# A two-layer decoder trunk on one core: half-height gate matmuls, weights loaded twice with a cast, and a spatial product of 256 columns

## The chip, the core and the metric

The kernel runs on one core of a Trainium2 chip. The metric is the device time of one execution, in microseconds (us). The kernel before was timed in three runs: 1560.33, 1560.44 and 1563.29 us, median 1560.44.

## What is computed

Two layers over x of 512 rows by 1024, in float32. Each layer adds half a SwiGLU feed-forward, a mixer, and half a second feed-forward, each behind an RMS norm. Layer 0 mixes with a recurrence, layer 1 with a spatial gate. Cut to the two mixers:

```python
def recurrent_mixer(x, w_in, conv_w, conv_b, ga_w, ga_b, gx_w, gx_b, lam, w_out):
    y, r = jnp.split(x @ w_in, 2, axis=-1)               # 1024 -> 2 x 1024
    y = jax.nn.gelu(y)
    r = causal_depthwise_conv(r, conv_w, conv_b)         # 4 taps
    gate_a = sigmoid(block_diag_linear(r, ga_w, ga_b))   # 16 heads of 64 x 64
    gate_x = sigmoid(block_diag_linear(r, gx_w, gx_b))
    log_a = -8 * gate_a * softplus(-lam)
    bx = r * gate_x * jnp.sqrt(-jnp.expm1(2 * log_a))
    h = scan(h[t] = exp(log_a[t]) * h[t-1] + bx[t])
    return (y * h) @ w_out

def spatial_gating_mixer(x, w_in, v_norm, w_s, b_s, w_out):
    u, v = jnp.split(jax.nn.gelu(x @ w_in), 2, axis=-1)
    v = rms_norm(v, v_norm)                              # 4 chunks of 128 rows, 8 heads of 128
    sg = jnp.einsum('hpq,bnqhc->bnphc', tril(w_s), vc) + b_s
    return (u * sg) @ w_out
```

## The kernel before, in words

`trunk` is written as one list of steps, the subs (`Sub`). A step takes one weight tile of 128x1024 from `rawp` (10 buffers, one load by SyncE, the SP queue), splits it into a high part `whi` (a copy by ScalarE, ACT, L117) and a low part `wlo` (a subtraction by VectorE, DVE, L108), and runs the tile's matmuls on TensorE, PE. Every product is three fp32r matmuls: high by high, high by low, low by high (`mm3`, L246 to L248, and `seven`, L481 to L483). `load_more` keeps the ten buffers filled, several steps ahead; a split runs three steps ahead of its matmuls (`SPLIT_AHEAD`). All other work is attached to a step by `hook(n, phase, fn)`, with the phases pre, mid, rest, end and late. Each engine executes its instructions in the order that results from this list. GpSimd (POOL) issues accumulating DMAs that add one weight block to another (L159).

**The recurrence** (`recurrent`). Steps r0 to r7 produce the channels of r, eight blocks of 128 rows by 512 columns; the first four are cut into halves of 256 columns. Steps y0 to y7 (`y0 = at0 + 12`) produce the channels of y. After each r step, `r_post` scales the product out of PSUM (`rc`, on ACT), adds three taps on DVE, and splits the result into `hi` (ACT) and `lo` (DVE). One or two steps later come the channel's gates: two blocks a and x, each a 128x128 weight tile with two 64x64 heads on its diagonal and zeros beside them, three matmuls of 512 columns each. Then two sigmoids of 128x512 and a tanh (ACT), and a product `pr` (DVE). `plan` places the rest: exponentials, `oma2`, square roots, scans, gelu, and `yh` = y * h, whose quarters form the left sides (A11, A12, S1 and so on) of the two groups of the output product `w_out`, which `seven` computes from seven block products P1 to Q4.

**The spatial mixer** (`spatial`). `prep_ws` loads the spatial weights 8 steps before the mixer and masks them (POOL); `tr_ws` turns them with eight PE transposes, and `take_ws` copies them out of PSUM (ACT). `v_norm` scales v with eight DVE operations of 128x512. `spat` multiplies: for each of 4 chunks and 2 halves of the heads four plain-float32 matmuls of 128 columns, 32 in all; the trace counts two passes for each. They stand in four groups of eight. `gated` adds the bias and multiplies by u.

Of the kernel before, what the change touches and what calls it, by code (L numbers as in the profile page):

```python
# [14 lines left out]
P = 128  # L15
# [21 lines left out]
SLOTS = 56  # L37

# [35 lines left out]
def trunk(ctx: ExitStack, tc: tile.TileContext, a: dict, out: bass.AP):  # L74
# [57 lines left out]
    class Raw:  # L132


        halves = False
# [36 lines left out]
    class Sub:  # L172
# [19 lines left out]
        def split(self, between=None):  # L192
# [4 lines left out]
            src = self.raw.v  # L197
            assert self.tile is None and self.raw.plus is None and self.raw.done == self.at[0]
# [1002 lines left out]
    def recurrent(w_in, w_out, norm):  # L1201
        gates = {}

        def load_gate(name, q):
            g = gates[name, q] = slot(name="gw")
            nc.gpsimd.memset(g, 0.0)
            gv = g.rearrange("p (c j) -> p c j", c=4)
            wv = a[f"rec_gate_{name}_w"][0, q * 8 : (q + 1) * 8].rearrange("(c two) i j -> two i c j", two=2)
            for two in range(2):
                nc.sync.dma_start(out=gv[two * 64 : (two + 1) * 64, :, two * 64 : (two + 1) * 64], in_=wv[two])  # L1210

        def split_gate(name, q):
            gates[name, q] = split(gates[name, q])
# [3 lines left out]
        for n, (name, q) in enumerate((name, q) for q in range(2) for name in ("a", "x")):  # L1217
            hook(at0 + (-9,-8,-2,-1)[n], "late", lambda name=name, q=q: load_gate(name, q))
            hook(at0 + (-3,-2,3,4)[n], "mid", lambda name=name, q=q: split_gate(name, q))
# [3 lines left out]
        def r_post(c, ps):  # L1223
            n = now[0]
            g = n + (2 if c < 4 or c == 6 else 1)
# [8 lines left out]
            def gate():  # L1234
                for name in "ax":
                    pg = bank("gate")
                    wh, wl = gates[name, c // 4]
                    cs = slice((c % 4) * P, (c % 4 + 1) * P)
                    mm3(pg, wh[:, cs], wl[:, cs], hl[0], hl[1], True, True)
                    pss.append(pg)  # L1240
                hl.clear()

            def sigmoids():
                for dst, brow in ((ga, V_GA), (gx, V_GX)):
                    dst[c] = slot(name="g")
                    act(dst[c], pss.pop(0), AF.Sigmoid, bias=vcol(brow + c))
# [8 lines left out]
            hook(n + 1, "mid", lambda: hl.extend(split(v)))  # L1255
# [53 lines left out]
        plan(-2, "rest", (exp_, 0, 1, 2, 3, 4), (oma2, 0, 1))  # L1309
# [31 lines left out]
        def mk(c0, post, halves):  # L1341

            raw = raw_of(w_in[:, c0 : c0 + P].rearrange("(k p) c -> p k c", p=P), [P, KD, P])
            st = {}
# [10 lines left out]
            last = lambda: post(st[0])  # L1355
# [22 lines left out]
    def spatial(w_in, w_out, norm):  # L1378
        wst, vg, v, sg = {}, {}, {}, {}
        ssv = cp.tile([P, 2 * TT], F32, tag="ssv", name="ssv")  # L1380

        def prep_ws():
            for q in range(2):
# [4 lines left out]
                                        fill=0.0, base=0, channel_multiplier=1)  # L1388
                vg[q] = slot(name="vg")
                nc.scalar.dma_start(out=vg[q], in_=a["sg_v_norm"][0, q * 512 : (q + 1) * 512].partition_broadcast(P))  # L1390
                wst[q] = w

        def tr_ws(q):
            ps = aux("wst")
            for i in range(4):
                nc.tensor.transpose(ps[:, i * P : (i + 1) * P], wst[q][:, i * P : (i + 1) * P], ident)
            wst[q] = ps

        def take_ws(q):
            wt = slot(name="wst")  # L1400
            act(wt, wst[q], AF.Copy)
            wst[q] = wt
# [58 lines left out]
        def v_norm(n):  # L1461
            for t in range(TT):
                stt(v[t, n], v[t, n], root["r"][:, t : t + 1], vg[n], ALU.mult, ALU.mult)

        def spat(t, n, where=None):

            ps = sg[t, n] = (where or aux)("sg")
            for i in range(4):
                c = slice(i * P, (i + 1) * P)
                nc.tensor.matmul(ps[:, c], wst[n][:, c], v[t, n][:, c], start=True, stop=True)  # L1470
# [8 lines left out]
        def gated(t, n):  # L1479
            ps, o = sg.pop((t, n)), hts[n][t]  # L1480
            for i in range(4):
                c = slice(i * P, (i + 1) * P)
                stt(o[:, c], ps[:, c], vcol(V_SB + n * 4 + i), o[:, c], ALU.add, ALU.mult)
            v.pop((t, n))
# [6 lines left out]
        hook(at0 - 8, "late", prep_ws)  # L1491
        for q in range(2):
            hook(at0 + 8 + q, "end", lambda q=q: tr_ws(q))
            hook(at0 + 9 + q, "mid", lambda q=q: take_ws(q))
# [5 lines left out]
        hook(u0 + 1, "mid", lambda: v_norm(0))  # L1500
        hook(u0 + 7, "mid", lambda: v_norm(1))
# [9 lines left out]
        for half, n, at, where in ((0, 0, 3, aux), (0, 1, 9, bank), (1, 1, 11, aux), (1, 0, 12, bank)):  # L1511
            for t in (2 * half, 2 * half + 1):
                hook(u0 + at, "end", lambda t=t, n=n, where=where: spat(t, n, where))
# [108 lines left out]
    def load_more(n=len(raws)):  # L1622
        nonlocal loaded
        while loaded < n and len(live) < RAW_BUFS:
# [181 lines left out]
```

## Time and profile before

| | |
|---|---|
| median of three runs | 1560.44 us |
| the profiled execution: its own time, and its span | 1560.53 us, 1558.5 us |
| PE busy | 1550.6 us, 99% of the span, 7277 matmuls |
| DVE busy | 1309.5 us, 84% |
| ACT busy | 1194.2 us, 77% |
| POOL busy | 244.5 us, 16% |
| granted TensorE clock | 1.0 |
| DMA | 311.58 MB, mean 200 GB/s |

A busy time counts the stretches in which at least one instruction of the engine is under way. Matmuls overlap, so a matmul's own duration (0.39 us for 512 columns) is longer than the step from one start to the next (0.23 us), and it is the step from start to start that one matmul adds to PE's time. The 40-slice picture of DMA use is lowest in three slices, 5, 3 and 3 tenths, at 142, 108 and 98 GB/s: these hold the recurrence.

### The profile page before, as it was taken

The numbers are of one execution on the slowest core, as the hardware profiler recorded it, in microseconds if no ns is written. First come the engines' busy times: TensorE is split into PE (matmuls) and PEld (weight loads), VectorE is DVE, ScalarE is ACT, GpSimd is POOL, SyncE is SP. The second block draws the span as 40 slices with busy tenths as digits, with TensorE's granted clock in tenths as the row PEclk, the third lists the DMA queues.
The fourth block names the chain that finished last, engine by engine and source line by source line (L and its number), as shares of the span: only waits on it lengthen the run. The fifth ranks groups of instructions, "written<-read, shape, count | busy, mean of one in ns | idle before, by whom it ended". The sixth has DMA issues, their size and how long they took to land.

```text
span 1558.5 us, 20998 instructions
## 1 busy us (share of the span) xinstructions
PE 1550.6 (99%) x7277; PEld 1317.1 (85%) x7277; DVE 1309.5 (84%) x1784; ACT 1194.2 (77%) x1785; POOL 244.5 (16%) x220
## 2 busy tenths in 40 slices
PE   9999999999999999999999999999999999999998
PEld 7888888898888998888889988888888889888886
DVE  6977789888999787789897877798979997777998
ACT  7877786668778868786787777867987877777856
POOL 2111112300021111112211111122211111111120
PEclk9999999999999999999999999999999999999999
DMA  9888898953395888899987887999978869898994
GB/s 316 187 189 192 188 219 223 232 142 108 98 236 136 191 198 198 187 235 223 232 209 180 191 203 185 230 218 235 252 191 216 203 140 218 197 206 184 241 232 137
DMA packets 272987, 311.58 MB, mean 200 GB/s; under 512 B 115456, under 2 KB 153456, under 8 KB 272880
## 3 DMA queue, kind: packets, MB, share of 16 engines
q1 hardware_dynamic: 218592, 211.06, 46.9%
q0 software_dynamic: 52496, 97.33, 37.1%
q10 hardware_dynamic: 1792, 1.84, 0.4%
q8 instruction: 57, 0.93, 0.2%
q14 instruction: 50, 0.41, 0.1%
HBM read 282.39 MB, written 2.10 MB: 183 GB/s over the span
## 4 chain that ended last, share of the span: by engine, by line
PE 98%; DVE 2%; DMA 0%; issue 0%; ACT 0%; DVEq 0%
PE A L483 15%; PE A L482 15%; PE A L481 15%; PE C L483 8%; PE C L481 8%; PE C L482 8%; PE B L482 4%; PE B L483 4%; PE B L481 4%; PE r L247 2%; PE r L248 2%; PE r L246 2%; PE Q L483 1%; PE Q L481 1%; PE Q L482 1%; PE p L961 1%
## 5 line engine op out<-in xcount | busy, mean ns | idle before, releaser
L108 DVE TENSOR_TENSOR wlo<-raw,whi 128x1024 fp32r<-128x1024 f32 (+2 forms) x567 | 651.1, 1152 | 210.6 <-ACT whi L117 207.0
L117 ACT ACTIVATE whi<-raw 128x1024 fp32r<-128x1024 f32 (+2 forms) x567 | 564.5, 1001 | 229.2 <-DVE raw L108 93.3
L481 PE MATMUL A<-whi,hi 128*128 128x512 f32 (+1 forms) x1104 | 420.8, 381 | 0.0
L482 PE MATMUL A<-whi,lo 128*128 128x512 f32 (+1 forms) x1104 | 419.3, 380 | 0.2 <-DVE lo L108 0.2
L483 PE MATMUL A<-wlo,hi 128*128 128x512 f32 (+1 forms) x1104 | 419.3, 380 | 0.0
L481 PEld LDWEIGHTS A<-whi,hi 128*128 128x128 f32 x1104 | 207.3, 188 | 35.9 <-ACT c L117 1.0
L482 PEld LDWEIGHTS A<-whi,lo 128*128 128x128 f32 x1104 | 207.3, 188 | 35.6 <-DVE lo L108 0.6
L483 PEld LDWEIGHTS A<-wlo,hi 128*128 128x128 f32 x1104 | 207.2, 188 | 35.7
L159 POOL DMA_DIRECT2D raw<-in_ffn_w_in_dram x100 | 120.7, 1207 | 708.8 <-DVE raw L108 322.8
L481 PE MATMUL C<-whi,hi 128*128 128x512 f32 (+1 forms) x608 | 231.5, 381 | 0.0
L483 PE MATMUL C<-wlo,hi 128*128 128x512 f32 (+1 forms) x608 | 231.3, 380 | 0.0
L482 PE MATMUL C<-whi,lo 128*128 128x512 f32 (+1 forms) x608 | 231.3, 380 | 0.0
L159 POOL DMA_DIRECT2D raw<-in_ffn_w_out_dram x73 | 83.8, 1189 | 319.0 <-DVE wlo L108 204.3
L108 DVE TENSOR_TENSOR raw<-raw,raw 128x1024 f32<-128x1024 f32 (+1 forms) x113 | 130.9, 1158 | 1.1
L482 PEld LDWEIGHTS C<-whi,lo 128*128 128x128 f32 x608 | 114.2, 188 | 20.2
L483 PEld LDWEIGHTS C<-wlo,hi 128*128 128x128 f32 x608 | 114.1, 188 | 19.9
L481 PEld LDWEIGHTS C<-whi,hi 128*128 128x128 f32 x608 | 114.1, 188 | 19.8
L117 ACT ACTIVATE c<-A 128x512 f32<-128x512 f32 (+1 forms) x150 | 81.8, 567 | 46.6 <-PE A L483 46.4
L108 DVE TENSOR_TENSOR lo<-a,hi 128x512 fp32r<-128x512 f32 (+1 forms) x180 | 116.3, 653 | 0.7 <-ACT hi L117 0.7
L117 ACT ACTIVATE hi<-a 128x512 fp32r<-128x512 f32 (+1 forms) x180 | 105.5, 596 | 14.4 <-DVE a L108 12.6
L482 PE MATMUL B<-whi,lo 128*128 128x512 f32 (+1 forms) x304 | 115.8, 381 | 0.0
L481 PE MATMUL B<-whi,hi 128*128 128x512 f32 (+1 forms) x304 | 115.7, 381 | 0.0
(190 smaller groups left out, 1973.5 us busy)
## 6 DMA issues: line engine op xcount, KB each, us to landing
raw<-in_ffn_w_in_dram SPq DMA_DIRECT2D x143, 512.0 KB, 5.5
raw<-in_ffn_w_out_dram SPq DMA_DIRECT2D x98, 512.0 KB, 5.7
raw<-in_ffn_w_in_dram POOLq DMA_DIRECT2D x76, 512.0 KB, 7.5
raw<-in_ffn_w_out_dram POOLq DMA_DIRECT2D x58, 512.0 KB, 8.4
raw<-in_ffn_w_in_dram SPq DMA_DIRECT2D x48, 384.0 KB, 4.0
raw<-in_sg_w_in_dram SPq DMA_DIRECT2D x20, 512.0 KB, 8.6
raw<-in_ffn_w_in_dram POOLq DMA_DIRECT2D x24, 384.0 KB, 6.4
raw<-in_rec_w_in_dram SPq DMA_DIRECT2D x16, 512.0 KB, 5.3
```

Of the source, the lines that this page charges most:

```text
L108: nc.vector.tensor_tensor(out=o, in0=x, in1=y, op=op)
L117: nc.scalar.activation(out=o, in_=x, func=f, **k)
L159: nc.gpsimd.dma_start(out=self.v, in_=src, accum_op=ALU.add)
L246: nc.tensor.matmul(ps, wh, xh, start=start, stop=False)
L247: nc.tensor.matmul(ps, wh, xl, start=False, stop=False)
L248: nc.tensor.matmul(ps, wl, xh, start=False, stop=stop)
L481: nc.tensor.matmul(ps, zh, wh, start=fresh and i == 0, stop=False, **k)
L482: nc.tensor.matmul(ps, zl, wh, start=False, stop=False, **k)
L483: nc.tensor.matmul(ps, zh, wl, start=False, stop=end, **k)
L961: nc.tensor.matmul(bank_of(half, s), z, (sub.lo if m == 2 else sub.hi)[:, q, :], start=left[2] == "2" and (h, q, m) == (0, 0, 0), stop=lef ...
```

## The change

Three edits, with two tables of places.

1. *Gates.* One tile holds, for four channels, gate a on the diagonal blocks and gate x on the off-diagonal blocks, so the POOL memsets go, and two tiles are split instead of four. The 64 rows of a head are now one matmul's whole contraction: per channel six matmuls of 64 rows by 128 columns of weights, 512 moving columns each, the two row halves alternating and each with a PSUM bank of its own. Four sigmoids of 64x512 replace two of 128x512. Gates run 3 steps after r0 to r3 and 2 steps after r4 to r7 (`GATE`). In `plan`, the first exponentials come one step later, the last three exponentials, square roots and scans later by a phase or two.
2. *Casting loads.* Each of the 12 unhalved weight tiles of the recurrence (r4 to r7, y0 to y7) is loaded a second time by a POOL DMA that casts it to fp32r. That is its high part; ACT makes no `whi`. Such a tile takes two of the ten buffers.
3. *Spatial.* The spatial weights are loaded and masked 90 steps before the mixer, and turned by `Group.send`: four ACT copies into planes, two transposing DMAs on SP, two ACT merges. `v_norm` writes tiles with two chunks side by side, in sixteen operations of 128x256, at `V_AT`; `spat` has 16 matmuls of 256 columns instead of 32 of 128.

```diff
+GATE = (3, 3, 3, 3, 2, 2, 2, 2)
+V_AT = 1, 7, 9, 10
+WS_AT, WS_MERGE = 90, 8
...
+            if self.cast:
+                self.h = rawp.tile([P, 1024], F32R, tag="raw", name=nm("rawhi")).rearrange("p (k c) -> p k c", k=k)
+                live.add((self, "hi"))
+                nc.gpsimd.dma_start(out=self.h, in_=self.src)
...
+            if self.raw.cast:
+                self.hi = self.raw.h
...
+                tt(self.lo, src, f32(self.hi), ALU.subtract)
...
-            g = n + (2 if c < 4 or c == 6 else 1)
+            g = n + GATE[c]
...
-                for name in "ax":
-                    pg = bank("gate")
-                    wh, wl = gates[name, c // 4]
-                    cs = slice((c % 4) * P, (c % 4 + 1) * P)
-                    mm3(pg, wh[:, cs], wl[:, cs], hl[0], hl[1], True, True)
-                    pss.append(pg)
+                pss.extend(bank("gate") for _ in range(2))
+                cs = slice((c % 4) * P, (c % 4 + 1) * P)
+                for m in range(3):
+                    for two in range(2):
+                        rows = slice(two * 64, (two + 1) * 64)
+                        nc.tensor.matmul(pss[two], gates[c // 4][m == 2][rows, cs], hl[0][m == 1][rows, :],
+                                         start=m == 0, stop=m == 2)
...
-                for dst, brow in ((ga, V_GA), (gx, V_GX)):
-                    dst[c] = slot(name="g")
-                    act(dst[c], pss.pop(0), AF.Sigmoid, bias=vcol(brow + c))
+                for dst, brow, n in ((ga, V_GA, 0), (gx, V_GX, 1)):
+                    g = dst[c] = slot(name="g")
+                    for two in range(2):
+                        o = (two ^ n) * 64
+                        act(g[two * 64 : (two + 1) * 64], pss[two][o : o + 64], AF.Sigmoid, bias=vcol(brow + c)[o : o + 64])
...
-        plan(-2, "rest", (exp_, 0, 1, 2, 3, 4), (oma2, 0, 1))
+        plan(-1, "rest", (exp_, 0, 1, 2, 3, 4), (oma2, 0, 1))
...
-        plan(1, "late", (exp_, 5, 6, 7), (oma2, 5, 6, 7))
-        plan(2, "rest", (sqrt, 5, 6, 7))
-        plan(2, "late", (gelu, 0, 1, 2), (scan, 5, 6, 7))
+        plan(2, "rest", (exp_, 5, 6, 7), (oma2, 5, 6, 7))
+        plan(2, "late", (sqrt, 5, 6, 7))
+        plan(2, "late", (gelu, 0, 1, 2))
+        plan(3, "rest", (scan, 5, 6, 7))
...
+            raw.cast = not halves
...
-                nc.tensor.transpose(ps[:, i * P : (i + 1) * P], wst[q][:, i * P : (i + 1) * P], ident)
...
+                g, cs = Group(2), slice(2 * k * P, 2 * (k + 1) * P)
+                pairs[k] = g
+                g.send("ws", lambda q, cs=cs: wst[q][:, cs], (now[0] + 1 + k, "mid"), (now[0] + WS_MERGE + k, "mid"))
...
-                nc.tensor.matmul(ps[:, c], wst[n][:, c], v[t, n][:, c], start=True, stop=True)
...
+                for i in range(2):
+                    nc.tensor.matmul(o[:, i], ws(n, 2 * j + i), x[:, i], start=True, stop=True)
...
-        while loaded < n and len(live) < RAW_BUFS:
+        while loaded < n and len(live) < RAW_BUFS - raws[loaded].cast:
```

PE, the gates of the first channel. Before, three matmuls into each of the two gate banks, one bank after the other:

```order
L246 MATMUL gate_3463<-hi_3394,hi_3112 128x512
L247 MATMUL gate_3463<-lo_3395,hi_3112 128x512
L248 MATMUL gate_3463<-hi_3394,lo_3113 128x512
L246 MATMUL gate_3467<-hi_3394,hi_3134 128x512
L247 MATMUL gate_3467<-lo_3395,hi_3134 128x512
L248 MATMUL gate_3467<-hi_3394,lo_3135 128x512
```

Now the two banks alternate, and one pair of weight tiles serves both:

```order
L1256 MATMUL gate_3481<-hi_3379,hi_3110 128x512
L1256 MATMUL gate_3482<-hi_3379,hi_3110 128x512
L1256 MATMUL gate_3481<-lo_3380,hi_3110 128x512
L1256 MATMUL gate_3482<-lo_3380,hi_3110 128x512
L1256 MATMUL gate_3481<-hi_3379,lo_3111 128x512
L1256 MATMUL gate_3482<-hi_3379,lo_3111 128x512
```

ACT, from the gates of channels 3 and 4 to the conv scaling (`rc`) of channel 7; `g` is a gate, `tl` the tanh. Before:

```order
L117 ACTIVATE g_3656<-gate_3628,vec 128x512
L117 ACTIVATE g_3658<-gate_3632,vec 128x512
L117 ACTIVATE tl_3660<-g_3656,lru_c 128x512
...
L117 ACTIVATE hi_3668<-rc_3644 128x512
L117 ACT_TABLE_LOAD
...
L117 ACTIVATE rc_3718<-r_3685,vec 128x512
L117 ACTIVATE whi_3723<-raw_3116 128x1024
```

In this excerpt from before, `rc_3718` is channel 6, and one more channel's sigmoids stand between it and channel 7. Now the scaling that follows the table load and the five exponentials is channel 7's, and no `whi` follows it:

```order
L120 ACTIVATE g_3678<-gate_3653,vec 64x512
L120 ACTIVATE g_3678<-gate_3654,vec 64x512
L120 ACTIVATE g_3681<-gate_3653,vec 64x512
L120 ACTIVATE g_3681<-gate_3654,vec 64x512
L120 ACTIVATE tl_3684<-g_3678,lru_c 128x512
...
L120 ACTIVATE hi_3694<-rc_3669 128x512
L120 ACT_TABLE_LOAD
...
L120 ACTIVATE rc_3746<-r_3713,vec 128x512
```

PE, the spatial product of one chunk before, with its four heads printed as one row:

```order
L1470 MATMUL sg_11026<-c_2298_10588,wst_10802 128x128 x4
```

and now the same four heads for two chunks, where `vp` is v with two chunks side by side:

```order
L1508 MATMUL sg_11031<-vp_10970,ws_8748 128x2x128 x2
L1508 MATMUL sg_11034<-vp_10973,ws_8768 128x2x128 x2
```

Twice as many columns stand in one matmul, and half as many matmuls in a group.

## Rows read from the trace of the kernel before

**Rows 1.** The page: busy time by engine, and the chain that ended last.

```profile
PE 1550.6 (99%) x7277; PEld 1317.1 (85%) x7277; DVE 1309.5 (84%) x1784; ACT 1194.2 (77%) x1785; POOL 244.5 (16%) x220
...
PE 98%; DVE 2%; DMA 0%; issue 0%; ACT 0%; DVEq 0%
```

**Rows 2.** Windows: us, busy us (x) of PE, PEld, DVE, ACT, POOL; clock, DMA share, GB/s.

```profile
340.00:380.50 40.50, 40.50 (x236) 35.82 (x236) 32.10 (x47) 31.79 (x50) 1.21 (x1) 1.00 0.34 94
380.50:441.00 60.50, 60.50 (x269) 50.09 (x268) 58.81 (x84) 43.84 (x59) 6.05 (x5) 1.00 0.47 115
441.00:457.00 16.00, 16.00 (x72) 13.26 (x71) 15.52 (x21) 9.56 (x14) 3.62 (x4) 1.00 0.94 213
```

**Rows 3.** Timeline of PE, first gate group: start us, us, engine, line, op, out<-in.

```profile
351.11 0.28 PE L247 MATMUL r<-zl,whi 128*128 128x256 f32 x1
...
351.35 0.40 PE L246 MATMUL gate<-hi,hi 128*128 128x512 f32 x1
352.50 0.39 PE L248 MATMUL gate<-hi,lo 128*128 128x512 f32 x1
352.73 0.28 PE L246 MATMUL r<-zh,whi 128*128 128x256 f32 x1
```

**Rows 4.** Timeline of PE, where r6 has ended.

```profile
377.46 0.39 PE L246 MATMUL gate<-hi,hi 128*128 128x512 f32 x1
```

**Rows 5.** Timeline of ACT, from the gates of channels 3 and 4 on.

```profile
371.13 1.25 ACT L117 ACTIVATE g<-gate,vec 128x512 f32<-128x512 f32 x2
372.27 0.73 ACT L117 ACTIVATE tl<-g,lru_c 128x512 f32<-128x512 f32 x1
372.88 1.27 ACT L117 ACTIVATE g<-gate,vec 128x512 f32<-128x512 f32 x2
...
374.64 0.64 ACT L117 ACTIVATE hi<-rc 128x512 fp32r<-128x512 f32 x1
375.30 1.28 ACT L117 ACT_TABLE_LOAD   x1
376.59 3.18 ACT L117 ACTIVATE g<-g,lru_nc 128x512 f32<-128x512 f32 x5
379.68 0.76 ACT L117 ACTIVATE rc<-r,vec 128x512 f32<-128x512 f32 x1
380.34 1.05 ACT L117 ACTIVATE whi<-raw 128x1024 fp32r<-128x1024 f32 x1
```

**Rows 6.** Timeline of DVE, where channel 7 begins.

```profile
383.83 1.29 DVE L108 TENSOR_TENSOR pr<-rc,g 128x512 f32<-128x512 f32 x2
...
385.80 2.32 DVE L114 SCALAR_TENSOR_TENSOR rc<-r,vec,rc 128x509 f32<-128x509 f32 x3
```

**Rows 7.** Timeline, left side S1 of the second output group.

```profile
440.15 0.68 DVE L108 TENSOR_TENSOR lo<-a,hi 128x512 fp32r<-128x512 f32 x1
...
441.61 0.39 PE L482 MATMUL C<-whi,lo 128*128 128x512 f32 x1
```

**Rows 8.** Timeline of PE, transposes of half the spatial weights.

```profile
1131.78 0.60 PE L1396 MATMUL wst<-ident,ws 128*128 128x128 f32 x4
...
1132.44 0.40 PE L482 MATMUL C<-whi,lo 128*128 128x512 f32 x1
```

**Rows 9.** Timeline of PE, one group of the spatial product.

```profile
1157.21 1.95 PE L1470 MATMUL sg<-c,wst 128*128 128x128 f32 x16
...
1159.22 0.40 PE L482 MATMUL C<-whi,lo 128*128 128x512 f32 x1
```

**Rows 10.** DMA issues: KB each, median us from issue to landing.

```profile
raw<-in_ffn_w_out_dram POOLq DMA_DIRECT2D x58, 512.0 KB, 8.4
...
raw<-in_rec_w_in_dram SPq DMA_DIRECT2D x16, 512.0 KB, 5.3
```

**Rows 11.** Lines by form, POOL: busy us, mean ns, idle before.

```profile
L159 POOL DMA_DIRECT2D raw<-in_ffn_w_in_dram x100 | 120.7, 1207 | 708.8 <-DVE raw L108 322.8
...
L1387 POOL TENSOR_SCALAR_AFFINE_SELECT ws<-ws 128x512 f32<-128x512 f32 x2 | 1.5, 760 | 13.1 <-DMA ws<-in_sg_w_s_dram 13.1
```

More of the change, by code (lines that the diff above doesn't have):

```diff
@@ L132, in trunk @@
     class Raw:
-        halves = False
+        halves = cast = False
         def __init__(self, src, shape, plus=None, wait=2):
@@ L1202, in recurrent, with load_gate, split_gate @@
         gates = {}
-        def load_gate(name, q):
-            g = gates[name, q] = slot(name="gw")
-            nc.gpsimd.memset(g, 0.0)
+        def load_gate(q):
+            g = gates[q] = slot(name="gw")
             gv = g.rearrange("p (c j) -> p c j", c=4)
[L1208 to L1213, printed above, removed]
+            for n, name in enumerate("ax"):
+                wv = a[f"rec_gate_{name}_w"][0, q * 8 : (q + 1) * 8].rearrange("(c two) i j -> two i c j", two=2)
+                for two in range(2):
+                    o = (two ^ n) * 64
+                    nc.sync.dma_start(out=gv[two * 64 : (two + 1) * 64, :, o : o + 64], in_=wv[two])
+        def split_gate(q):
+            gates[q] = split(gates[q])
         at0 = len(subs)
         y0 = at0 + 12
-        for n, (name, q) in enumerate((name, q) for q in range(2) for name in ("a", "x")):
-            hook(at0 + (-9,-8,-2,-1)[n], "late", lambda name=name, q=q: load_gate(name, q))
-            hook(at0 + (-3,-2,3,4)[n], "mid", lambda name=name, q=q: split_gate(name, q))
+        for q in range(2):
+            hook(at0 + (-9, -2)[q], "late", lambda q=q: load_gate(q))
+            hook(at0 + (-3, 3)[q], "mid", lambda q=q: split_gate(q))
         rc, ga, gx, tl, pr, ym = {}, {}, {}, {}, {}, {}
@@ L1254, in r_post @@
             hook(n, "late", taps)
[L1255 removed]
+            hook(n + 1, "mid", lambda: hl.append(split(v)))
             hook(g, "end", gate)
@@ L1353, in mm_of, with last @@
                 return mm
-            last = lambda: post(st[0])
+            def last():
+                live.discard((raw, "hi"))
+                post(st[0])
             if not halves:
@@ L1378, in spatial @@
     def spatial(w_in, w_out, norm):
-        wst, vg, v, sg = {}, {}, {}, {}
+        wst, vg, v, sg, pairs, vp = {}, {}, {}, {}, {}, {}
         ssv = cp.tile([P, 2 * TT], F32, tag="ssv", name="ssv")
@@ L1490, in spatial @@
         at0 = len(subs)
[L1491 to L1494, printed above, removed]
+        hook(at0 - WS_AT, "late", prep_ws)
+        hook(at0 - 8, "late", load_vg)
+        hook(at0 - WS_AT + 6, "late", planes_ws)
         seven_chunk(D, v_done, ((2, 3), (3, 4), (2, 3)))
@@ L1499, in spatial @@
         hook(u0 + 1, "pre", v_newton)
-        hook(u0 + 1, "mid", lambda: v_norm(0))
-        hook(u0 + 7, "mid", lambda: v_norm(1))
+        for (half, n), at in zip(((0, 0), (0, 1), (1, 1), (1, 0)), V_AT):
+            hook(u0 + at, "mid", lambda half=half, n=n: v_norm(half, n))
         def drop(name):
@@ L1511, in spatial @@
         for half, n, at, where in ((0, 0, 3, aux), (0, 1, 9, bank), (1, 1, 11, aux), (1, 0, 12, bank)):
+            hook(u0 + at, "end", lambda half=half, n=n, where=where: spat(half, n, where))
             for t in (2 * half, 2 * half + 1):
-                hook(u0 + at, "end", lambda t=t, n=n, where=where: spat(t, n, where))
                 hook(u0 + at + 2, "mid", lambda t=t, n=n: gated(t, n))
@@ L1655, in vec_rest @@
             flat = src.rearrange("h d -> (h d)") if len(src.shape) == 2 else src.rearrange("o h d -> (o h d)")
-            nc.gpsimd.dma_start(out=stage[r0 : r0 + n, :P], in_=flat.rearrange("(n p) -> n p", p=P))
+            v = flat.rearrange("(n p) -> n p", p=P)
+            if r0 == V_GX:
+                for o in (0, 64):
+                    nc.gpsimd.dma_start(out=stage[r0 : r0 + n, o : o + 64], in_=v[:, 64 - o : 128 - o])
+            else:
+                nc.gpsimd.dma_start(out=stage[r0 : r0 + n, :P], in_=v)
     def vec_rest_t():
```

56 lines of the change are left out of this document (36 added, 20 removed).

## Prediction

> **What bounds the kernel now.** I read the page first. PE is busy for 99% of the span, and the chain that ended last is 98% PE [rows 1]: the reader is to see that, over the whole, an instruction taken from PE's queue is time taken from the kernel. But that is an average over stages, and the largest edit lies in one of them. So I cut the recurrence into windows [rows 2]. From 340 to 380.5 us DVE is busy for 32.10 of 40.50 us; from 380.5 to 441 for 58.81 of 60.50, and then until 457 for 15.52 of 16.00. PE never stops there, but DVE is at 97%. So two engines set the pace side by side in the second half of the recurrence, and the margin between them decides what a faster PE is worth. I take the margin from the timeline at the end of that stretch [rows 7]: the `lo` of the block S1 of the second output group starts on DVE at 440.15 and lasts 0.68, so it is there at 440.83; PE reads it at 441.61. The margin is 0.78 us. This is the number on which the forecast turns.
>
> **Gates on PE.** Each channel's six matmuls run from 351.35 to 352.73 [rows 3]: 1.38 us, 0.23 each. Now they are three pairs, and the halves of a pair use different rows of the array and different PSUM banks. No row of this trace shows such a pair. The bounds: together, a pair takes one matmul's 0.23; one after the other, 0.46. I take 0.24, near the lower end, because the two halves share neither weights, nor moving rows, nor a bank. Then a channel takes 0.72 instead of 1.38, and eight channels give back 5.3 us of PE's queue. Against it stands the overhang of a matmul: the last of the group lasts 0.39 but is followed after 0.23 [rows 3]. If the array had to empty wherever 128-row and 64-row matmuls meet, each meeting would cost up to that 0.16; there are seven places with gates in the new order, so 14 meetings and 2.2 us.
>
> **What becomes of the 5.3 us.** They are saved before and inside the stretch that DVE paces, so I follow DVE's work. Its last long run starts with the taps of channel 7 at 385.80 [rows 6] and goes on without a gap of note to the end of that `lo` at 440.83: 55.0 us. The new order has the same operations in this run and two more products `pr`, since the products of channels 6 and 7 now come after the taps. Two of them were 383.83 to 385.13, by their 1.29 us less the overlap about 0.6 each [rows 6], so 1.2 us more. So the question is when the taps of channel 7 start. They need its scaling `rc` on ACT, which lasts 0.76 [rows 5], so it must start some 0.8 us before them. The new order puts that `rc` directly behind this run on ACT: four sigmoids and a tanh of channel 3, the same of channel 4, `hi`, a table load, five exponentials. The run starts with the gates of channel 3, which stand behind r6. r6 ended at 377.46 [rows 4], behind five channels' gates; now three stand before it, so it ends at 377.46 - 5 x 1.38 + 3 x 0.72 = 372.7, and the gates of channel 3 are out of PE at 372.7 + 0.72 + 0.16 = 373.6. The durations from ACT's starts [rows 5]: a sigmoid 0.57 (371.13 to 372.27 is two), the tanh 0.61, `hi` 0.66, the table load 1.29, five exponentials 3.09. A sigmoid over 64 partitions has the same 512 columns, and I give it the same 0.57. Sum: 2 x (4 x 0.57 + 0.61) + 0.66 + 1.29 + 3.09 = 10.8, so `rc` of channel 7 starts at 384.4 and the taps at 385.2, 0.6 earlier than before. Then 385.2 + 55.0 + 1.2 = 441.4 for the `lo` of S1, against the 441.61 at which PE read it before. PE arrives 5.3 us earlier, at about 436.3, and **waits some 5 us**. What the recurrence gains is about 0.2 us, and behind it DVE is still at 97% [rows 2], so PE cannot run ahead there either.
>
> The rest of this edit: ACT gets 16 sigmoids more (9.2 us) and loses 12 `whi` of some 0.95 to 1.05 us [rows 5], 12 us. Nothing beside the run above hangs on it. DVE loses two splits of gate tiles, before 380.5, where it had 8.4 us to spare [rows 2]: nothing. The POOL memsets wait for nobody. The exponentials and scans of channels 5 to 7 are among the operations counted.
>
> **Casting loads.** They take `whi` from ACT, and DVE keeps its `wlo`, so DVE's stretch is not shortened. Their cost is in queues. An SP load of a tile of this stage lands in 5.3 us, an accumulating load that POOL issues in 8.4 [rows 10], at an issue of 1.2 us [rows 11]. A casting load lies between these two or above. It is issued about six steps ahead and needed at the split, three steps ahead; a step has 24 matmuls of 0.23 [rows 3], 5.5 us, so there are 16 us. DMA has room there, a share of 0.34 and 0.47 [rows 2]. Cost nothing; the cover ends where a cast takes over 16 us.
>
> **Spatial weights.** Four transposes on PE lie between 1131.78 and the second matmul behind them, 1132.44 [rows 8]; take off that first matmul's 0.23, and they cost 0.43. Twice that goes: **-0.87 us**, on PE's own queue in a stage where PE sets the pace. The masked load moves 82 steps ahead; POOL waited 13.1 us for its two loads there already [rows 11], with no step of the chain on POOL [rows 1], so I price the same wait in the same kind of feed-forward at nothing. ACT has six operations for two, at 0.6 to 1.05 each by its rows [rows 5] some 2.4 to 4.2 us over a whole feed-forward layer in which it is idle for a quarter: nothing.
>
> **Spatial product.** A group of 16 passes runs from 1157.21 to 1159.22 less 0.23 [rows 9]: 1.78 us, 0.111 a pass; four groups, 7.1 us. Afterwards there are 32 passes of 256 columns. The lower bound is a 256-column pass of fp32r, 0.12 (351.11 to 351.35 is two) [rows 3]: 32 x 0.12 = 3.8, a gain of 3.3. The upper bound is twice today's pass: 32 x 0.222 = 7.1, no gain. A pass of 128 plain float32 columns lasts as long as nearly 256 of fp32r, so plain float32 goes at half the rate by columns, and I take **zero**. The scaling of v is split into 16 operations of half the width: on DVE's rows of 128x512, 0.68 [rows 7], at most 5.4 us more, over a stage of ten steps of the mixer; DVE is idle for 16% overall [rows 1]. Nothing.
>
> A rule speaks for more. The Trainium skill ("TensorE: Matmul & The Clock Gate", LDWEIGHTS) says that loading weights of P columns takes about P/1.2 ns; by an estimate from that page, 107 ns for 128 columns, and the trace's 0.111 a pass agrees with it. By that rule the load sets the pace of today's passes, and the sum would be 1556.2 rather than 1559.5; rival 2 works it out from rows.
>
> **Sum.** The profiled execution took 1560.53 us: 1560.53 - 0.87 (transposes) - 0.2 (recurrence) - 0 (casts) - 0 (product) = 1559.46. It stands 0.09 above the median of the three runs, so the forecast is **1559.5 us**.
>
> **Rivals.**
>
> 1. *DVE's margin is larger than I read it*, since DVE's order also changes, and the `wlo` of 12 tiles no longer wait for an ACT copy. For it: DVE has 1.7 us idle between 380.5 and 441 [rows 2]. Against it: its run from 385.80 has no room for 5 us. Then PE's whole saving counts: 1560.5 - 5.3 - 0.9 = 1554.3. Chance 0.13.
> 2. *The weights' load sets the pace of a spatial pass.* A pass then costs its weights' load, whatever its columns; the 256-column pass costs 0.12 [rows 3], and 3.3 us go: 1556.2. For it: the transposes, with one pass each, step at the same 0.11 [rows 8]. Against it: 512 columns of fp32r take 0.23 and 256 take 0.12 [rows 3], and the same loads at 0.12 give half the columns in plain float32. Chance 0.10.
> 3. *The 64-row matmuls cost more.* If the array empties at each meeting, r6 ends and the gates come out 7 x 0.16 = 1.1 later (the gates of channels 0 to 2 and the entry to channel 3), the taps and the `lo` of S1 too: 442.5, 0.9 behind 441.61, and 1560.53 + 0.9 - 0.9 = 1560.5. If the pairs run one after the other, r6 ends at 377.46 - 2 x 1.38 = 374.7, the first gates are out at 376.2, 2.6 later than forecast, the `lo` of S1 at 444.0, 2.4 behind: 1562.1. The Trainium skill ("TensorEngine Tiling (Array Packing)", Key Properties) says that a change of the tiling mode drains TensorE; no row of the trace shows a change of mode. Chance 0.13 for both.
> 4. *Slower: the casting loads are late.* Each takes a POOL issue and two of ten buffers, and the twelve come one after another on one queue. The point is 16 us from issue to landing, or 5.5 us of POOL per load. Beyond that each step waits: at 1 us in each of the eight y steps, where DVE has no room to make it up, 1559.5 + 8 = 1567.5. For it: POOL's own loads land later than SP's [rows 10]. Against: 8.4 us is half of 16, and DMA stands at less than half. Chance 0.06.
>
> **How the numbers follow.** The forecast has 0.58, with a range of its own from 1558.6 to 1560.5 (half of DVE's 1.7 us of idle time on one side, an ACT run that is a tenth longer than 10.8 us on the other). A measurement of this kernel can tell 0.2%, 3.1 us, from no change. Rivals 1 and 2 lie below 1557.3: faster 0.23. Rival 4 lies above 1563.6, and so does a small part of rival 3: slower 0.07. Within: 0.70. The range leaves out rivals 1 and 4, 0.19 in all, and takes in 2 and 3: 1556.0 to 1562.3.
>
> **What would show it.** Each step has its row in the changed kernel's trace: a gate group on PE that takes some 0.72 us for a channel; r6's end near 372.7; the taps of channel 7 near 385.2; waits of PE in the last y step and in the first products of the output, summing to 4 to 5 us, ended by DVE; the read of S1 near 441.4; no `wst` transposes; a spatial group of 1.78 us. The forecast is wrong if PE reads S1 of the second group before 440, if the waits of PE end on a DMA, or if a spatial group takes a microsecond.

## The result, and the profile after

The changed kernel takes 1563.75 us, median of 19 runs (1561.68 to 1572.66), against 1560.52 for the kernel before (19 runs, 1559.89 to 1563.29): a ratio of 1.0027, 95% interval 1.0018 to 1.0035. It is slower by 4.2 us by the ratio, 3.2 by the medians. The forecast was 1559.5, its range ended at 1562.3, and slower had a chance of 0.07. The profiled execution took 1565.62 us, its span is 1563.9.

First the page of the changed kernel: busy time, and the chain that ended last.

```profile
PE 1550.4 (99%) x7237; PEld 1310.4 (84%) x7237; DVE 1309.2 (84%) x1790; ACT 1197.0 (77%) x1791; POOL 253.5 (16%) x229
...
PE 89%; DVE 6%; ACT 2%; DMA 1%; issue 1%; POOL 0%; DVEq 0%; POOLq 0%; ACTq 0%
```

PE is busy for as long as before [rows 1], and the span is 5.4 us longer. The chain, 98% PE before, now has 6% DVE and 2% ACT in it. The waits of PE in the changed kernel say where (engine, tile, line, what it waited for: us in total, times, longest):

```profile
PE r L262 <- DVE wlo L111: 2.1, 1, 2.1
PE C L495 <- ACT hi L120: 1.7, 1, 1.7
...
PE Q L495 <- ACT whi L120: 0.9, 1, 0.9
PE C L496 <- DVE lo L111: 0.6, 1, 0.6
PE Q L497 <- DVE wlo L111: 0.5, 1, 0.5
```

`r L262` is step y7, `C` is the block with S1. Waits were forecast at both places, 4 to 5 us in all and ended by DVE, and they come to 4.3 us. The longer of the two at S1 ends on ACT, whose `hi` had itself waited for DVE, as the timeline below shows. Two things were not forecast. The windows, as [rows 2]:

```profile
340.00:380.50 40.50, 40.50 (x243) 34.04 (x242) 31.91 (x44) 27.63 (x44) 4.38 (x5) 1.00 0.58 121
380.50:441.00 60.50, 58.43 (x260) 46.28 (x259) 54.83 (x79) 46.51 (x65) 6.66 (x7) 1.00 0.71 176
441.00:457.00 16.00, 13.75 (x53) 10.65 (x52) 14.51 (x20) 8.04 (x11) 5.86 (x5) 0.89 1.08 246
```

DVE is *less* busy in the second half, 54.83 us against 58.81: it was waiting for ACT at the start of that stretch, and its work slid past 441. Its rows there show it (in brackets the idle time before an instruction, and what ended it); the last is the taps of channel 7:

```profile
382.38 0.69 DVE L111 TENSOR_TENSOR lo<-rc,hi 128x512 fp32r<-128x512 f32 x1 [3.58 <-ACT hi L120]
...
384.41 0.69 DVE L111 TENSOR_TENSOR a<-g 128x512 f32<-128x512 f32 x1 [1.34 <-ACT g L120]
...
387.53 2.32 DVE L117 SCALAR_TENSOR_TENSOR rc<-r,vec,rc 128x509 f32<-128x509 f32 x3 [0.37 <-ACT rc L120]
```

And the granted clock of the last window is 0.89. The timeline at S1:

```profile
442.46 0.63 ACT L120 ACTIVATE hi<-a 128x512 fp32r<-128x512 f32 x1 [1.17 <-DVE a L111]
...
443.14 0.50 PE L495 MATMUL C<-whi,hi 128*128 128x512 f32 x1 [1.67 <-ACT hi L120]
...
443.48 0.68 DVE L111 TENSOR_TENSOR lo<-a,hi 128x512 fp32r<-128x512 f32 x1
...
444.22 0.73 PE L496 MATMUL C<-whi,lo 128*128 128x512 f32 x1 [0.57 <-DVE lo L111]
...
444.75 0.63 PE L497 MATMUL C<-wlo,hi 128*128 128x512 f32 x1
...
445.18 0.63 PE L495 MATMUL C<-whi,hi 128*128 128x512 f32 x1
```

The `lo` of S1 is there at 444.16, not 441.4; PE reads it at 444.22, where before it read it at 441.61 [rows 7]. And after the two waits the matmuls step by 0.43 us instead of 0.23: the half clock, 1.2 GHz (the granted clock is 0.50 from 445 to 447 us).

Compared matmul by matmul with the trace of before, the changed kernel is 0.2 us ahead at the entry of the recurrence, 2.7 ahead from 400 to 420 us, 2.9 *behind* at the third matmul of S1, and 4.3 behind when the half clock ends. The spatial mixer gives back 0.7 (4.2 behind at 1126, 3.4 at 1200). The last 2.0 come at 1518, in the waits of `Q` above. Such waits stand in the traces of three of the six kernels taken here that have all three edits, and in none of the other thirteen changed kernels; so they go with some executions of the change and not with all. The profiled execution is 1.9 us above the median.

### The profile page after: what moved, and what is told of

Same layout as the page of the kernel before. It is cut to its first block, busy times and chain, and to the rows that moved or that the text cites. A ratio compares the mean times of both kernels' runs of the same rounds, so it can differ in the third digit from the quotient of the medians.

```text
span 1563.9 us, 20971 instructions
## 1 busy us (share of the span) xinstructions
PE 1550.4 (99%) x7237; PEld 1310.4 (84%) x7237; DVE 1309.2 (84%) x1790; ACT 1197.0 (77%) x1791; POOL 253.5 (16%) x229
## 4 chain that ended last, share of the span: by engine, by line
PE 89%; DVE 6%; ACT 2%; DMA 1%; issue 1%; POOL 0%; DVEq 0%; POOLq 0%; ACTq 0%
PE A L496 15%; PE A L495 15%; PE A L497 15%; PE C L496 8%; PE C L497 8%; PE C L495 8%; PE B L496 4%; PE B L497 4%; PE B L495 4%; DVE wlo L111 2%; PE p L975 1%; PE Q L497 1%; PE Q L496 1%; PE Q L495 1%; DMA raw<-in_ffn_w_out_dram 1%
## 5 line engine op out<-in xcount | busy, mean ns | idle before, releaser
L111 DVE TENSOR_TENSOR wlo<-raw,whi 128x1024 fp32r<-128x1024 f32 (+2 forms) x555 | 636.6, 1151 | 212.9 <-ACT whi L120 210.7
L120 ACT ACTIVATE whi<-raw 128x1024 fp32r<-128x1024 f32 (+2 forms) x555 | 551.6, 1000 | 230.3 <-DVE raw L111 91.9
```

Of the source, the lines that this page charges most:

```text
L111: nc.vector.tensor_tensor(out=o, in0=x, in1=y, op=op)
L120: nc.scalar.activation(out=o, in_=x, func=f, **k)
```

## The experiments

**Which edit it is.** Each edit alone, and the changed kernel without the gates; "alone" takes the hunks of the diff shown above that belong to it.

```diff
+V_AT = 1, 7, 9, 10
+WS_AT, WS_MERGE = 90, 8
...
```

> The kernel before with the spatial edit alone (weights turned by transposing DMAs, 16 matmuls of 256 columns). Theory: only the eight transposes count, 0.9 us off PE's queue, the product itself costs the same 7.1 us; 1559.6 us. Rival, the extra waits behind VectorE that the changed kernel shows near 1127, 1139, 1162 and 1180 us (0.2 us each) come from this edit and eat the gain: 1560.4 to 1561.

Measured: 1559.18 (10 runs), 1.2 us under the 1560.41 of before on its chip. The median is where the theory put it, but the interval of the ratio, 0.9983 to 1.0002, still allows no gain.

```diff
+GATE = (3, 3, 3, 3, 2, 2, 2, 2)
...
```

> The kernel before with the gate edit and its plan alone, no casting loads. Theory (ScalarE's and VectorE's run to the block S1 is late, and PE's idle time there costs the clock): PE saves some 2.4 us on its queue, but the read of S1 moves from 441.6 to 444 us or later, and the half clock behind it costs 2 us: 1564 to 1566 us. Rival (the casting loads cost the time): without them the 2.4 us are saved, 1558 us.

Measured: 1572.87 (4 runs), 12.5 us slower, more than twice what I expected. PE waits 3.4 us for a `whi` and 1.9 for a `hi`, both on ACT, and the granted clock is 0.50 from 397 to 403 and from 434 to 437 us.

```diff
+            raw.cast = not halves
...
```

> The kernel before with the casting loads alone. Theory: they change nothing that sets the end, since VectorE's work stays: 1560.2 to 1560.7 us, no wait of PE over 0.5 us in the recurrence. Rival (casting loads land late or load the queues): PE waits in the y steps for VectorE's wlo, 1563 us.

Measured: 1559.92 (10 runs) against 1560.41, the same; no wait of PE in the recurrence. The casting loads land in 5.3 us, median.

```diff
-GATE = (3, 3, 3, 3, 2, 2, 2, 2)
...
```

> The changed kernel with the gates, their order and the plan put back; casting loads and spatial edit stay. Theory: 1559.6 us, clock 1.0 throughout, no wait at S1. Rival (casting loads cost the time): 1563 us.

Measured: median 1560.62, lowest 1558.82, but 1564.7, 1564.8 and 1568.7 among 10 runs. The lowest fits the theory; the spread fits neither, and comes back below.

So the gates cost the time, and the casting loads give most of it back: they take 12 `whi` from ACT, and without them the gates cost 12 us. By the waits, what the gate edit is short of is ACT.

**Does DVE's run set S1?**

```diff
-            tt(pr[c], pr[c], tl.pop(c), ALU.mult)
+            tl.pop(c)
```

> The changed kernel without the product of pr by the square root ahead of each scan (8 operations of 0.7 us on VectorE, between the taps of channel 7 and S1); the recurrence then runs on other numbers. Theory (VectorE's run to S1 sets the pace): the lo of S1 comes 5.6 us earlier, at 438.6, ahead of PE, no wait and no half clock there; PE's own saving shows, 1560.5 - 2.4 - 0.9 = 1557.2 us. Rival (PE's gate groups or the DMA set it): the time stays within 1 us of the changed kernel's 1563.7.

Measured: lowest 1558.31, median 1561.01 with the same spread (four of ten runs over 1566), so the time itself is not told from the kernel before. In the trace the third matmul of S1 is 0.8 us *ahead* of the kernel before, 3.7 earlier than in the changed kernel. VectorE's run did set it. PE still waits 1.1 us there, since ACT's `hi` is next in line; so 3.7 came of the 5.6.

**Is it the order of the steps?**

```diff
-GATE = (3, 3, 3, 3, 2, 2, 2, 2)
+GATE = (2, 2, 2, 2, 1, 1, 2, 1)
...
-        plan(-1, "rest", (exp_, 0, 1, 2, 3, 4), (oma2, 0, 1))
+        plan(-2, "rest", (exp_, 0, 1, 2, 3, 4), (oma2, 0, 1))
...
```

> The changed kernel with the places of gates and plan as before (gates two or one steps behind r, first exponentials one step earlier); matmuls, sigmoids, casting loads and spatial edit stay. Theory (the long run of ScalarE ahead of the scaling of channel 7 is what makes S1 late): that scaling follows r7 at once, the taps start by 384.5, and S1 by 440.5; the wait is under 1 us, the clock stays, 1557.5 to 1559 us. Rival (the half-height gates are dear wherever they stand): 1562 us or more.

Measured: 1563.97, and S1 is 2.7 us late, against 2.9 in the changed kernel. PE now waits in front of the gates, 2.0 us for `hi` on ACT and 1.3 for `lo`. The rival holds: the lateness moves with the order, it does not go.

**Is it the sigmoids, or PE's changes of tile size?** The run of ACT ahead of channel 7, in the changed kernel:

```profile
373.94 0.78 ACT L120 ACTIVATE rc<-r,vec 128x512 f32<-128x512 f32 x1 [1.20 <-PE r L262]
374.83 2.81 ACT L120 ACTIVATE g<-gate,vec 64x512 f32<-64x512 f32 x4
377.67 0.72 ACT L120 ACTIVATE tl<-g,lru_c 128x512 f32<-128x512 f32 x1
378.30 2.78 ACT L120 ACTIVATE g<-gate,vec 64x512 f32<-64x512 f32 x4
381.10 0.72 ACT L120 ACTIVATE tl<-g,lru_c 128x512 f32<-128x512 f32 x1
...
386.74 0.76 ACT L120 ACTIVATE rc<-r,vec 128x512 f32<-128x512 f32 x1
```

Four sigmoids take 2.84 us from start to start, 0.71 each; two full ones took 1.14 [rows 5]. And PE's gates in the changed kernel, of one channel (367.27) and of two in a row (373.83):

```profile
367.27 0.50 PE L1256 MATMUL gate<-hi,hi 64*128 64x512 f32 x2
367.61 0.40 PE L1256 MATMUL gate<-lo,hi 64*128 64x512 f32 x2
367.84 0.39 PE L1256 MATMUL gate<-hi,lo 64*128 64x512 f32 x2
...
373.83 0.50 PE L1256 MATMUL gate<-hi,hi 64*128 64x512 f32 x2
...
381.08 0.50 PE L1256 MATMUL gate<-hi,hi 64*128 64x512 f32 x2
```

The halves of a pair do run together: 0.23 a pair (367.61 to 367.84). From 367.27 to 373.83 are 6.56 us, with 24 matmuls of 0.2275 in between: 1.10 for the channel. From 373.83 to 381.08, with two channels, 1.79. So a channel takes 0.69 and each visit to the gates 0.41 more, 0.2 for each change of tile size, from 128 rows to 64 and back. Eight channels in seven visits take 8.4 us, not 5.8; PE saves 2.6.

Two kernels tell the two apart. Both leave the spatial mixer as it was, so their base is the kernel with the gate edit and the casting loads alone:

```diff
+            raw.cast = not halves
...
+GATE = (3, 3, 3, 3, 2, 2, 2, 2)
```

> The kernel before with the gate edit and the casting loads, spatial mixer as before. Theory (recurrence late by 2.6 us at S1, half clock behind it 1.9, and the executions at 1570 us and more come from the spatial weights' transposing DMAs at 90 steps ahead): the changed kernel without its 0.9 us of gain, lowest 1562.5, median 1564, and no execution over 1568. Rival (the spread comes from the recurrence): executions of 1570 and more remain.

Measured: median 1564.32, 1562.95 to 1565.14, 10 runs. As the theory said, and no long executions.

```diff
-                    for two in range(2):
-                        o = (two ^ n) * 64
-                        act(g[two * 64 : (two + 1) * 64], pss[two][o : o + 64], AF.Sigmoid, bias=vcol(brow + c)[o : o + 64])
+                    act(g, pss[n], AF.Sigmoid, bias=vcol(brow + c))
```

> Gate edit and casting loads, spatial mixer as before, with two sigmoids of 128x512 per channel instead of four of 64x512; each reads a whole bank, so its gates mix heads and the recurrence runs on other numbers. Theory (the half-height sigmoids, 0.71 us a start and four of them, lengthen ScalarE's run ahead of channel 7 by 1.7 us for each of two channels): the taps start at 384.1 and the lo of S1 at 440.7, ahead of the 441.6 of before; S1 costs nothing, PE waits 1 to 2 us, 1560 us against 1564.3 with four sigmoids. Rival (the changes of tile size on PE are what is late): 1563.5 or more.

Measured: 1559.36 (10 runs), 5.0 us under the base and 1.7 under the 1561.03 of before on its chip, ratio 0.9989 (0.9979 to 0.9998). Its ACT timeline:

```profile
375.26 0.78 ACT L120 ACTIVATE rc<-r,vec 128x512 f32<-128x512 f32 x1 [2.76 <-PE r L262]
376.16 1.27 ACT L120 ACTIVATE g<-gate,vec 128x512 f32<-128x512 f32 x2
377.31 0.72 ACT L120 ACTIVATE tl<-g,lru_c 128x512 f32<-128x512 f32 x1
...
384.71 0.76 ACT L120 ACTIVATE rc<-r,vec 128x512 f32<-128x512 f32 x1
```

From `rc` to `rc` 9.45 us instead of 12.80 in the changed kernel, and S1 is level with the kernel before. The changes of tile size are still in this kernel, so they alone do not make it slower.

```diff
-                for m in range(3):
-                    for two in range(2):
-                        rows = slice(two * 64, (two + 1) * 64)
-                        nc.tensor.matmul(pss[two], gates[c // 4][m == 2][rows, cs], hl[0][m == 1][rows, :],
+                for two in range(2):
+                    for m in range(3):
+                        nc.tensor.matmul(pss[two], gates[c // 4][m == 2][:, cs], hl[0][m == 1],
                                          start=m == 0, stop=m == 2)
```

> Gate edit and casting loads, spatial mixer as before, with the six gate matmuls of a channel over all 128 rows, one bank after the other; both banks then hold sums over two heads and the recurrence runs on other numbers. Order, places and sigmoids stay. A channel takes PE 1.37 us instead of 1.11, alone, or 0.9, as one of two. Theory (PE's gates matter little, the sigmoids much): r6 ends 0.8 us later, S1 0.8 to 1.2 later, 1565 to 1565.5 us. Rival (the changes of tile size are what is late): without them 1561 us.

Measured: 1564.35, the base's time. Giving back the whole gain on PE costs nothing that shows, since PE waits less, and taking away the changes of tile size gains nothing. This run does not show what those changes cost by themselves, since its gates take longer without them: counted from the entry of the recurrence, S1 comes 0.5 us later than in the base. But with full sigmoids the time comes back and with full rows it does not. It is the sigmoids that decide.

```diff
-                for dst, brow, n in ((ga, V_GA, 0), (gx, V_GX, 1)):
-                    g = dst[c] = slot(name="g")
-                    for two in range(2):
+                ga[c], gx[c] = slot(name="g"), slot(name="g")
+                for two in range(2):
+                    for dst, brow, n in ((ga, V_GA, 0), (gx, V_GX, 1)):
+                        g = dst[c]
```

> The changed kernel with the four sigmoids of a channel in another order: first halves of both gates, then second halves, so that no two in a row write one tile. Theory (a sigmoid that writes the tile of the one before it waits for its end, 0.71 us a start instead of 0.57): starts 0.57 apart, the run of ScalarE ahead of channel 7 shorter by 1.1 us, S1 at 443.0, and with the shorter wait the time 1 to 2 us less, 1562 us. Rival (half-height sigmoids cost 0.71 by themselves): no change.

Measured: 1564.36, and four sigmoids still take 2.81 us. The theory falls: the 0.71 is not a wait for the tile's first half. It goes with the 64-row form; why, no run here shows.

**What the half clock costs.**

```diff
+                        if order[:3] == [("P1", 0), ("P5", 0), ("P2", 0)] and (prod, ci, s) == ("P1", 1, 1) and end:
+                            for _ in range(12):
+                                nc.tensor.matmul(ps, warm[:, :P], warm[:, :w], start=False, stop=False, **k)
```

> The changed kernel with 12 matmuls of zeros by zeros added into the bank of the block A just before its last matmul, where PE would wait for S1; the sums stay as they are. The wait is 1.84 + 0.85 us, the fillers last 12 x 0.23 = 2.7. Theory (the wait costs the clock as well as itself): the granted clock stays at 1.0 from 443 to 448 us, the read of the lo of S1 stays near 444.2, and the time falls by 1.9 us. Rival (the half clock has another cause, such as the drains of the gate groups): it stays, and the time does not fall.

Measured: 1569.48, 1561.65 to 1576.92. In its trace the half clock stands at 425 to 428, behind the wait in y7, so PE was late already and the fillers made it 1 us later. This run settles nothing, so both waits were filled:

```diff
+                        if c0 == 7 * P and k == KORDER[0]:
...
+                            for _ in range(10):
+                                nc.tensor.matmul(st[0][:, t], warm[:, :P], warm, start=False, stop=False)
```

> The kernel of the run before this one with PE's two waits filled: 10 matmuls of zeros by zeros into the bank of y7 ahead of its first wlo, 12 ahead of S1. Theory (the half clock follows the waits): granted clock 1.0 from 420 to 450 us, no wait over 0.5 us there, and the time 1.9 us less than without the fillers. Rival (half clock from the drains at the gates): it stays, and the time is the same or more.

Measured: 1563.92, 1562.6 to 1567.15; S1 is 3.0 us late by its third matmul, in the base's profile 2.6. The windows of the filled kernel:

```profile
410.00:430.00 20.00, 20.00 (x89) 15.43 (x88) 19.07 (x30) 10.92 (x17) 1.21 (x1) 1.00 0.79 211
430.00:450.00 20.00, 20.00 (x88) 15.00 (x88) 20.00 (x32) 12.37 (x17) 6.04 (x5) 1.00 0.99 222
```

and of its base:

```profile
410.00:430.00 20.00, 17.91 (x73) 14.33 (x72) 19.07 (x30) 10.93 (x16) 1.21 (x1) 0.91 0.78 210
430.00:450.00 20.00, 19.17 (x84) 15.34 (x83) 20.00 (x32) 12.01 (x18) 6.05 (x5) 1.00 0.99 226
```

Without waits there is no half clock: that half of the theory holds. But the time falls by 0.4 us, not 1.9. In the base's profile the half clock stood behind y7, and the wait at S1 swallowed it, because VectorE sets S1 (its window is full, 20.00 of 20.00) whatever PE does. In the changed kernel's profile it stood behind S1 and cost 1.4 us. How often it falls where is not known from one profile a kernel.

**The long executions.** 3 of 19 runs of the changed kernel took over 1570 us, and 11 of 30 in three of the kernels above that have its gates and its spatial edit (fillers, sigmoids in turn, old order). The kernels with less work on VectorE and without the gates are some us faster, so a fixed line hides their long runs; counted from each kernel's own lowest run, 4 of 10 and 1 of 10 of theirs are more than 7 us above it, and two more of the latter 5.9; of 150 runs of the kernel before, one is. None of 40 with its gates and the spatial mixer of before was over 1568 (the base, both waits filled, full sigmoids, full rows), and none of 10 with the spatial edit alone over 1562. One of the long ones has a profile, that of the old order. Its SP queue, ahead of a wait of PE of 7.4 us:

```profile
907.38 4.48 SPq L163 DMA_DIRECT2D raw<-in_ffn_w_in_dram  x3
913.15 15.27 SPq L347 DMA_TRANSPOSE dt<-pl  x2
```

and ACT, which merges the spatial weights between two splits:

```profile
915.30 1.17 ACT L120 ACTIVATE ws<-dt 128x1024 uint16<-128x1024 uint16 x1
922.28 1.06 ACT L120 ACTIVATE whi<-raw 128x1024 fp32r<-128x1024 f32 x1 [5.82 <-DMA raw<-in_ffn_w_in_dram]
```

From 893 to 926 us the loads there took 18.0 us to land, in the changed kernel's own profile 4.3. The transposes of the spatial weights stand just ahead of the feed-forward's own, and in this execution the loads between them are held up. A mild form stands in the profile of the spatial edit alone: PE waits 0.7 us at 918 for ACT, and the loads from 893 to 926 took 5.9 us to land. So I moved the transposes.

```diff
-WS_AT, WS_MERGE = 90, 8
+WS_AT, WS_MERGE = 34, 8
```

> The changed kernel with the spatial weights loaded and turned 34 steps ahead of the mixer instead of 90, where the feed-forward sends no transposes of its own. Theory (the transposes of the spatial weights stand among the feed-forward's own and hold up weight loads on the same queue in about a quarter of the executions): no execution above 1569 us, lowest 1561.7, median 1563. Rival (the spread is the casts' or the chip's): a quarter of the executions still above 1569.

Measured: 1571.33 (7 runs), 1565.34 to 1575.16.

The same edit without gates and casting loads:

> The kernel before with the spatial edit alone, its weights turned 34 steps ahead. Theory: the 0.9 us of the transposes and no spread: 1559.2 us, lowest 1558.9, no execution above 1561. Rival (34 steps ahead collides as well): executions some us above.

Measured: 1567.31 (6 runs), 1561.68 to 1570.6. Both theories fall, and the second rival holds: 34 steps ahead is worse even without gates and casting loads. PE waits 4.1 us near 1056 here and 6.1 near 1062 in the run before, each time behind a `hi` on ACT that stands after a late weight load. Two more places, the same line with 300 and 104:

> The kernel before with the spatial edit alone, its weights turned 300 steps ahead, at the entry of the recurrence, where DMA is at a third of its use. Theory (the transposing DMAs cost only where loads are dense): 1559.3 us, no execution above 1562. Rival (they hold up loads anywhere, or ScalarE's extra work delays the recurrence): 1561 or more.

Measured: 1559.27, 1558.7 to 1562.3, against 1561.03 of before; two runs of ten are at 1562.2 and 1562.3.

> The same with the weights turned 104 steps ahead, in the last steps of the feed-forward before. Theory: loads are dense there, some executions 2 to 8 us longer, 1560 to 1567 us. Rival (only the neighbourhood of the feed-forward's own transposes hurts): 1559.3 us.

Measured: 1562.05, 1558.75 to 1564.41. The place decides: at the entry of the recurrence nothing is held up. But the theory's reason, that loads are sparse there, fails. With the weights turned 300 steps ahead, the two transposes stand at

```profile
315.52 3.67 SPq L336 DMA_TRANSPOSE dt<-pl  x2
```

and in the kernel before the windows of this place and of the ones 104, 90 and 34 steps ahead are (columns as [rows 2], DMA's share the last but one):

```profile
305.00:320.00 15.00, 15.00 (x76) 12.66 (x75) 12.73 (x23) 10.90 (x20) 2.56 (x5) 1.00 0.97 229
860.00:885.00 25.00, 25.00 (x146) 25.00 (x146) 17.53 (x23) 18.08 (x30) 4.82 (x4) 1.00 0.92 232
885.00:926.00 41.00, 41.00 (x184) 34.06 (x183) 31.61 (x35) 31.11 (x45) 4.82 (x4) 1.00 0.87 194
1030.00:1056.00 26.00, 26.00 (x117) 21.52 (x116) 26.00 (x33) 18.14 (x28) 5.49 (x5) 1.00 0.92 213
```

The share of 0.34 in [rows 2] begins only at 340 us, behind the transposes. So what makes one place good and another bad stays open. It also stays open why the place of the changed kernel hurt in 18 of 59 runs with the gates, in 1 to 3 of 10 with the casting loads and no gates, and in none of 10 alone; whether the casting loads have a part in it, no run settles. Then the good place for longer, and with the casting loads:

> The kernel before with the spatial edit alone, weights turned 300 steps ahead, a second time and longer, for the interval: 0.9 to 1.2 us under the kernel before, 0.06 to 0.08%. Rival (no gain that holds): within 0.5 us.

Measured: 1560.05 (11 runs) against 1561.1 (21 runs): ratio 0.9993, 0.9984 to 1.0002.

> The same with the casting loads, gates as before. Theory (casting loads alone change nothing or some 0.3 us; turning the weights ahead of the recurrence avoids the dense loads): as the run without them or 0.3 us less, no execution over 1563. Rival (casting loads and the transposes meet at the entry of the recurrence): executions some us longer.

Measured: 1559.84, one execution of 1564.86 in 11; ratio 0.9993 as well. Both are some 1 us under the kernel before and 4 under the changed one; against the kernel before, the interval still allows no gain. The casting loads add nothing without the gates.

## Why the prediction was wrong

*The bound.* Right. DVE's run to S1 with a margin of 0.78 us decided, PE's gain on its own queue became a wait, and the waits stand where they were put, at y7 and at S1, with 4.3 us. Taking 5.6 us from that run moved S1 by 3.7.

*Pairs on PE.* The pair is right: 0.23, with 0.24 forecast. Each meeting of 128-row and 64-row matmuls costs 0.2 us; I had put it at 0 in the sum and at 0.16 in rival 3. The Trainium skill's rule that a change of tiling mode drains TensorE ("TensorEngine Tiling (Array Packing)", Key Properties) agrees with the trace, at 0.2 us a change. The meetings moved r6's end to 373.7 instead of 372.7, and with 0.2 more to the first sigmoid that is 1.2 us of the error, as read from the trace; no run isolates it.

*The sigmoids.* **The step that failed** is the start of the taps of channel 7, 385.2 in the sum and 387.53 in the trace. The meetings of tile sizes, put at nothing, are the first part of that error. The second is this: "A sigmoid over 64 partitions has the same 512 columns, and I give it the same 0.57." It takes 0.71, and eight of them in the run of ACT are 1.1 us. I priced a new form by the nearest row. The forecast's own range, to 1560.5, allowed for a run of ACT that is a tenth longer, which is these 1.1 us, so this term alone would have stayed inside it; it left the range together with the meetings and with the price of being late, below. That there are four sigmoids instead of two was in the sum; together, count and price are 3.4 us of that run, and taking both away gave 5.0. No run changes the price alone.

*The run from the taps.* 55.0 + 1.2 were forecast, 56.6 measured (387.53 to 444.16): right but for a gap of 0.7 us in which DVE waited for `hi` on ACT. Sum: 441.4 + 1.2 + 1.1 + 0.4 = 444.1.

*The price of being late.* I took PE's wait for free, as time that it had saved. Behind S1 the wait was followed by the half clock, 1.4 us in the profile. No term of the sum and no rival had that. With S1 2.8 us later than forecast the sum comes to 1562.3, the end of the stated range, and with the half clock to 1563.7. That this meets the measured 1563.75 so closely is in part luck, since other profiles show the half clock elsewhere or not at all.

*Casting loads.* They cost nothing, as forecast (4.8 us to land in the changed kernel, 16 available). But I called ACT's 12 us beside the point: without them the gates cost 12.5 us. So rival 4, the slower side, was sought in the loads, and it lay in the engine that they relieve.

*Spatial edit.* For the transposes 0.87 was forecast; from 1126 to 1200 us the changed kernel gains 0.7 on the kernel before. The product: a group of 8 passes of 256 columns in the changed kernel,

```profile
1160.87 1.89 PE L1508 MATMUL sg<-vp,ws 128*128 128x256 f32 x8
...
1162.83 0.39 PE L496 MATMUL C<-whi,lo 128*128 128x512 f32 x1
```

takes 1.73 us (1160.87 to 1162.83 less 0.23), against 1.78 [rows 9], 0.216 a pass: zero, as forecast, and rival 2 is out. The 107 ns for 128 columns of weights, an estimate from the Trainium skill ("TensorE: Matmul & The Clock Gate", LDWEIGHTS), are not what paced a pass: the trace disagrees with that reading, since twice the moving columns doubled it. What I priced at nothing and should not have is the transposes' *place*: on SP's queue, among the feed-forward's own. The executions above 1570 us go with it, and the one that has a profile shows the loads held up there.

*Rival 1*, that DVE's margin is larger, is out. *Rival 3* had the right direction and one of the causes, the meetings of tile sizes; its other case, pairs one after the other, did not occur.

## What to carry to other kernels

When an instruction is cut into halves over partitions, price the halves by a row of that very form or give the price an upper bound. Here each half cost 0.71 us against 0.57 for the whole, with twice as many of them, and a run on ACT that nobody waited for became the one that all wait for. Where PE's gain ends behind an engine that is 97% busy, ask what a later arrival on that engine costs, not only what an earlier one on PE brings. Try several places for a small transposing DMA: at one its gain was kept, at others some executions lost ten times as much, and DMA's share of use did not tell the good place from the bad.

## What the runs showed that I had not expected

A sigmoid of 64x512 starts 0.71 us after the one before it, one of 128x512 after 0.57, though both last about 0.69: the half-height ones do not overlap, the full ones do. Writing other tiles in turn does not change it (2.81 us for four).

A change between 128-row and 64-row matmuls costs 0.2 us each way, in seven visits 2.9 us of the 5.5 that the pairs save.

The half clock came after waits of PE of about 2 us, behind S1 in the changed kernel and behind y7 in the base, for 3 to 4 us each time. It did not come behind y7 in the changed kernel, where the wait was as long (2.1), nor in the kernel with full rows, whose waits at S1 were as long as the changed kernel's (1.7 and 0.6), nor in the kernel whose waits were filled with matmuls of zeros. What decides between them, no run here shows.
